# A hybrid attention block on one core: the MLP's two-operand work moves to VectorE, squares to ScalarE, and what is spilled to DRAM is laid out anew

## The chip, the cores and the metric

The kernel runs on one core of one Trainium2 chip. The metric is the device time of one execution in microseconds (us), lower is better. Five engines matter: TensorE (PE in the profile, its weight loads PEld), VectorE (DVE), ScalarE (ACT), GpSimd (POOL) and SyncE (SP), which issues nearly all DMA transfers. Each works through its own queue in order and waits on semaphores for the others.

## What is computed

A sequence of 1024 rows of width 1024 goes through one layer in float32: a mixer (sparse attention heads and gated DeltaNet heads), and then an MLP with a norm on either side. The change lies in the MLP and in the turning of its input:

```python
D_MODEL = 1024; SEQ = 1024; D_FF = 4 * D_MODEL
def rms_norm(x, g):
    y = x * lax.rsqrt(jnp.mean(x * x, axis=-1, keepdims=True) + EPS)
    return y * g
...
    x = x + rms_norm(mix, post_norm_mix[l])
    h = rms_norm(x, pre_norm_mlp[l])
    y = jnp.square(jax.nn.relu(h @ w_mlp_in[l])) @ w_mlp_out[l]
    x = x + rms_norm(y, post_norm_mlp[l])
```

## The kernel before

Products are made of split numbers: a float32 operand becomes a high part (a cast to a shorter type, by ScalarE) and a low part (what the cast left, a subtraction by VectorE or GpSimd, `parts`, L1414 to L1421), and one product is three matmuls, high by high, high by low, low by high (`mm3`, L192 to L201).

**The input turned.** `turn_h2` (L1365) takes each block of 128 rows of x after the mixer, multiplies it by its row's factor (L1375), turns it with eight transposes into two PSUM banks, and writes high and low parts of h, the norm's weight being applied per partition in the same step (L1386, L1387). h lies transposed in `h2H` and `h2L`. It is one of several generators that a small planner (`Flow`) interleaves with the end of the mixer; the blocks come from the last to the first. The order on each engine's queue is then set by a scheduler that simulates the program, and not by the order of the text alone.

**Four plain blocks.** 4 of the 32 blocks of 128 hidden columns are done plainly (`plain`, L1472): 24 matmuls for each half of the rows, a squared Relu (`squared`, L1465), a write to DRAM.

**28 blocks in 14 pairs.** The others go through a scheme of seven products of blocks in place of eight. It needs sums and differences of the four quarters of h: `turns_of_h` (L1487) adds high and low parts of h back together in spare tiles, forms three combinations (b11, b22, b21) with their high and low parts in `TH` and `TL`, and a fourth that replaces a half of h. The first loop (L1559) takes the pairs in turn. For each, `left_parts` (L1522) forms the four sums of weight quarters and the parts of seven left sides, at most three or four combinations ahead; then, in the order 1, 5, 6, 2, 7, 3, 4, come 12 matmuls a combination, and the results are added up, squared and combined. Seven blocks of 256 KB a pair are written to `hid_d` (`spill`).

The second loop (L1686) multiplies these by w_mlp_out. It takes the pairs in chunks of 2, 3, 3, 3 and 3, and for each chunk the combinations 1, 2, 5, 3, 6, 7, 4: a step. `both_parts` (L1635) reads the hidden blocks into spare tiles, forms the differences of weight quarters, and makes the parts of both sides, in rings of 12 buffers (`hq` for the hidden side, `hl` for the weights). A step of a triple is 36 matmuls, four row blocks t by three pairs, and after each row block `gather` (L1676) adds a PSUM bank to an accumulator. Raw weights of a chunk (1 MB a pair) are loaded at the chunk's start. Most of the memory of the second loop is that of h and its sums, so `room` (L1617) opens it when the first loop is through.

At the end the accumulator u is added to three others (L1714), the four plain blocks are multiplied (L1735), and `finish` norms each row block and adds x.

## Time and profile before

| | |
|---|---|
| median of 3 runs | 1456.03 us (1451.3 to 1461.72) |
| the profiled execution | 1456.56 us, its span 1454.9 us |
| instructions | 20267 |
| TensorE busy | 1310.5 us, 6643 matmuls |
| VectorE busy | 1102.6 us |
| ScalarE busy | 684.0 us |
| GpSimd busy | 754.3 us |
| mean granted clock of TensorE | 0.945 of full |
| DMA | 180.29 MB, mean 124 GB/s |

The span runs from the first to the last instruction of one execution; places in it are given in us from its start. Busy shares are means over the whole span. The MLP's products run from about 763 us (beside the end of the mixer) to 1437 us. A stretch is judged by how many matmuls it issues, since a matmul's busy time overlaps with the next one's.

### The profile page before, as it was taken

The numbers are of one execution on the slowest core, as the hardware profiler recorded it, in microseconds if no ns is written. First come the engines' busy times: TensorE is split into PE (matmuls) and PEld (weight loads), VectorE is DVE, ScalarE is ACT, GpSimd is POOL, SyncE is SP. The second block draws the span as 40 slices with busy tenths as digits, with TensorE's granted clock in tenths as the row PEclk, the third lists the DMA queues.
The fourth block names the chain that finished last, engine by engine and source line by source line (L and its number), as shares of the span: only waits on it lengthen the run. The fifth ranks groups of instructions, "written<-read, shape, count | busy, mean of one in ns | idle before, by whom it ended". The sixth has DMA issues, their size and how long they took to land. (4 is left out here: it accounts for less than half of the span.)

```text
span 1454.9 us, 20267 instructions
## 1 busy us (share of the span) xinstructions
PE 1310.5 (90%) x6643; PEld 1120.7 (77%) x6643; DVE 1102.6 (76%) x2350; ACT 684.0 (47%) x1475; POOL 754.3 (52%) x625
## 2 busy tenths in 40 slices
PE   7898997988876999999989599999994999999995
PEld 5687885877765999878877488888883888887874
DVE  5524759998997898997786957777776877767946
ACT  5433336777632677776464333333331443434422
POOL 3163320222233434348011846777663999899973
PEclk8999998999985999999999799999997999999998
DMA  6222112555163332334435124444447645543015
GB/s 186 69 70 80 44 30 58 172 150 127 44 165 103 102 92 72 113 109 153 148 130 174 46 96 156 159 152 156 152 155 278 236 125 172 181 129 110 30 55 177
DMA packets 159939, 180.29 MB, mean 124 GB/s; under 512 B 26129, under 2 KB 113370, under 8 KB 159706
## 3 DMA queue, kind: packets, MB, share of 16 engines
q1 hardware_dynamic: 159834, 179.00, 39.2%
q8 instruction: 52, 0.85, 0.3%
q14 instruction: 53, 0.43, 0.1%
HBM read 120.76 MB, written 59.78 MB: 124 GB/s over the span
## 5 line engine op out<-in xcount | busy, mean ns | idle before, releaser
L199 PE MATMUL two<-hTH,wh 128*128 128x512 f32 (+1 forms) x416 | 165.9, 401 | 26.0 <-ACT tmp L424 16.0
L200 PE MATMUL two<-hTL,wh 128*128 128x512 f32 (+1 forms) x416 | 166.1, 399 | 0.0
L201 PE MATMUL two<-hTH,wl 128*128 128x512 f32 (+1 forms) x416 | 164.8, 397 | 0.0
L1420 POOL TENSOR_TENSOR hq<-tmp,hq 128x512 fp32r<-128x512 f32 x96 | 143.9, 1513 | 9.8 <-ACT hq L1419 8.4
L1420 POOL TENSOR_TENSOR hl<-raw,hl 128x512 fp32r<-128x512 f32 x67 | 100.7, 1513 | 51.9 <-ACT hl L1419 51.9
L1419 ACT CAST hq<-tmp 128x512 fp32r<-128x512 f32 x96 | 59.1, 617 | 128.3 <-POOL hq L1420 67.0
L269 POOL TENSOR_SCALAR wh<-stg 128x1024 fp32r<-128x1024 f32 x19 | 19.9, 1046 | 191.1 <-PE two L200 191.1
L199 PEld LDWEIGHTS two<-hTH,wh 128*128 128x128 f32 (+1 forms) x416 | 81.8, 197 | 43.6 <-issue 22.7
L521 ACT ACTIVATE jk<-score,cand 128x1024 bf16<-128x1024 f32 (+2 forms) x96 | 92.5, 966 | 45.1 <-DVE cand L532 31.4
L1419 ACT CAST hl<-tmp 128x512 fp32r<-128x512 f32 x58 | 35.6, 618 | 160.7 <-DVE tmp L1535 60.9
L201 PEld LDWEIGHTS two<-hTH,wl 128*128 128x128 f32 (+1 forms) x416 | 81.6, 196 | 12.7 <-issue 0.9
L200 PEld LDWEIGHTS two<-hTL,wh 128*128 128x128 f32 (+1 forms) x416 | 81.8, 197 | 12.0 <-issue 0.7
L270 POOL TENSOR_TENSOR wl<-stg,wh 128x1024 fp32r<-128x1024 f32 (+1 forms) x26 | 60.8, 2340 | 54.1 <-ACT wh L267 52.6
L1134 POOL TENSOR_TENSOR mt<-tz,maskb 128x256 f32<-128x256 f32 x56 | 38.4, 691 | 60.4 <-DVE mx L1150 39.6
L1158 ACT ACTIVATE big<-big,nm 128x256 f32<-128x256 f32 (+6 forms) x64 | 50.6, 791 | 12.5 <-DVE nm L1157 12.5
L199 PE MATMUL acc<-h2H,hl 128*128 128x512 f32 x120 | 47.5, 400 | 9.1 <-DVE tmp L1469 9.1
L1419 ACT CAST hl<-raw 128x512 fp32r<-128x512 f32 x88 | 52.8, 615 | 5.4 <-PE acc L200 4.9
L1184 DVE TENSOR_TENSOR part<-tr,part 128x512 fp32r<-128x512 f32 x80 | 50.2, 630 | 4.9 <-ACT part L1183 4.6
L1183 ACT CAST part<-tr 128x512 fp32r<-128x512 f32 x80 | 43.2, 542 | 20.6 <-PE tr L1181 17.1
L200 PE MATMUL acc<-h2L,hl 128*128 128x512 f32 x120 | 47.7, 398 | 4.5 <-DVE h2L L1387 4.5
L1206 PE MATMUL acc<-part,VS 128*128 128x256 f32 x288 | 49.4, 295 | 1.3 <-DVE part L1184 1.2
L587 DVE SCALAR_TENSOR_TENSOR tmp<-two,svT,tmp 128x1023 f32<-128x1023 f32 (+2 forms) x36 | 45.5, 1276 | 4.0 <-ACT tmp L585 3.0
(516 smaller groups left out, 4385.7 us busy)
## 6 DMA issues: line engine op xcount, KB each, us to landing
hid_d<-tmp SPq DMA_DIRECT2D x98, 256.0 KB, 2.0
tmp<-hid_d SPq DMA_DIRECT2D x98, 256.0 KB, 2.7
raw<-in_w_mlp_in_dram SPq DMA_DIRECT2D x14, 1024.0 KB, 8.2
raw<-in_w_mlp_out_dram SPq DMA_DIRECT2D x14, 1024.0 KB, 5.1
stg<-in_w_in_dram SPq DMA_DIRECT2D x25, 512.0 KB, 4.1
x<-in_x_dram SPq DMA_DIRECT2D x8, 512.0 KB, 5.5
la_d<-la SPq DMA_DIRECT2D x8, 512.0 KB, 3.7
q<-qa_d SPq DMA_DIRECT2D x64, 64.0 KB, 2.4
```

The source lines that it names most:

```text
L199: PE.matmul(o, lh, rh, start=start, stop=False, skip_group_check=more)
L200: PE.matmul(o, lh, rl, start=False, stop=False, skip_group_check=more)
L201: PE.matmul(o, ll, rh, start=False, stop=stop, skip_group_check=more)
L270: G.tensor_sub(wl[:, :, :n], f[:, :, :n], wh[:, :, :n].bitcast(F32))
L521: S.activation(junk[:, :n], s_of(b), AF.Sign, bias=cand[:, 3 + i:4 + i].bitcast(F32), scale=-1.0, accum_out=cnt[:, 3 + i:4 + i])
L587: V.scalar_tensor_tensor(acc[:, 3 - j:T], both[:, 0:T - 3 + j], w[j], acc[:, 3 - j:T], op0=OP.mult, op1=OP.add)
L1158: S.activation(pr[:, :n], pr[:, :n], AF.Exp, bias=nm, accum_out=den[:, hh:hh + 1])
L1183: S.copy(pt[:, 0:2 * nj, 0, :], v4(ps)[:, 0:2 * nj])
L1184: V.tensor_sub(pt[:, 0:2 * nj, 1, :], v4(ps)[:, 0:2 * nj], pt[:, 0:2 * nj, 0, :].bitcast(F32))
L1206: PE.matmul(po[:, hh * 256:hh * 256 + 256], VS[:, j + a, 2 * p + hh, :], pt[:, 2 * a + hh].rearrange("p a t -> p (a t)"), start=j + a + hh ...
L1419: S.copy(h_, src)
L1420: eng.tensor_sub(l_, src, h_.bitcast(F32))
```

## The change

Names of the parts, in the order of the text:

- `turn_h2`: the norm's weight is applied to rows, ahead of the transposes, in one operation with two tensor inputs on VectorE (a tile `gain` holds the weights in every partition). Parts are then taken from four transposed blocks at once. A plain copy of them, `hf`, is made by ScalarE and written to DRAM, in four tiles (two halves of the columns by two halves of the rows).
- `turns_of_h` reads these blocks from DRAM in place of adding high and low parts; its low parts go to VectorE.
- `squared` and the other squares: Relu and then Square on ScalarE.
- Every `parts`, addition and subtraction of the two loops and of the closing rows that was on GpSimd goes to VectorE, with the first three plain weight loads and `finish` left as they were.
- `hid_d`: one DRAM tile for each pair and combination; combinations 1, 2 and 4 are split before they are written, high and low part, and read straight into the ring `hq` (`hl` for the very first).
- Raw weights of the next chunk are loaded at combinations 3 and 6 of the current one, and the third after it.
- The additions of u come within the last chunk, after combinations 6, 7 and 4, row block by row block.

```diff
@@ -1372,20 +1372,19 @@
             yield flow.now + 3.0
-        V.tensor_scalar(xr, xr, r2[:, tb:tb + 1], None, op0=OP.mult)
-        yield dve(flow.now, 1.1)
+        V.scalar_tensor_tensor(xr, xr, r2[:, tb:tb + 1], h2["gain"], op0=OP.mult, op1=OP.mult)
+        yield dve(flow.now, 1.3)
...
             yield from bank("tr")
...
-            for k in range(4):
-                kk = kh * 4 + k
-                ts_ = slice(tb * P, (tb + 1) * P)
-                gn = svT[:, 57 + kk:58 + kk]
-                S.activation(h2["H"][:, kk, ts_], ps[:, k * P:(k + 1) * P], AF.Identity, scale=gn)
-                V.scalar_tensor_tensor(h2["L"][:, kk, ts_], ps[:, k * P:(k + 1) * P], gn,
-                                       h2["H"][:, kk, ts_].bitcast(F32), op0=OP.mult, op1=OP.subtract)
+            kk, ts_ = slice(4 * kh, 4 * kh + 4), slice(tb * P, (tb + 1) * P)
+            S.copy(h2["H"][:, kk, ts_], v4(ps))
+            V.tensor_sub(h2["L"][:, kk, ts_], v4(ps), h2["H"][:, kk, ts_].bitcast(F32))
+            hf = pl.t(h2["hf"], H4, F32, "hf", bufs=2)
+            S.copy(hf, v4(ps))
+            SY.dma_start(h2["d"][kh][tb // 4][:, :, tb % 4 * P:tb % 4 * P + P], hf)
...
             yield 0.0
@@ -1406,6 +1405,10 @@
+h2["hf"], hf_close = pl.open("hf")
+h2["gain"] = pl.t(h2["hf"], [P, D], F32, "gmlp")
+SY.dma_start(h2["gain"], bcast(pre_norm_mlp, P))
+h2["d"] = [[pl.t(dram, [P, 4, 512], F32, f"h2_d{i}{j}") for j in range(2)] for i in range(2)]
@@ -1420,13 +1423,13 @@
-def load_plain(f, stage, **kw):
+def load_plain(f, stage, eng, **kw):
...
-    mlp[f] = [parts(raw[:, 4 * k:4 * k + 4, :], G) for k in range(2)]
+    mlp[f] = [parts(raw[:, 4 * k:4 * k + 4, :], eng) for k in range(2)]
...
-    load_plain(f, pool["wk"], bufs=2)
+    load_plain(f, pool["wk"], G, bufs=2)
@@ -1434,6 +1437,7 @@
+hf_close()
@@ -1448,8 +1452,9 @@
-hid_d = pl.t(dram, [NP2, 7, P, 512], F32, "hid_d")
-plain_d = pl.t(dram, [NS, P, T], F32, "plain_d")
+hid_d = {(i, j): pl.t(dram, [P, 512], F32, f"hid{i}_{j}") for i in range(NP2) for j in range(3, 7)}
+hid_d.update({(i, j): pl.t(dram, [P, 2, 512], F32, f"hid{i}_{j}") for i in range(NP2) for j in range(3)})
+plain_d = [pl.t(dram, [P, T], F32, f"plain{f}") for f in range(NS)]
...
 def tmp(dtype=F32):
@@ -1466,12 +1471,12 @@
-    V.scalar_tensor_tensor(r, ps, 0.0, r, op0=OP.max, op1=OP.mult)
+    S.activation(r, r, AF.Square)
...
 def plain(f, th):
...
-        load_plain(f, stg)
+        load_plain(f, stg, V)
@@ -1479,25 +1484,24 @@
-    SY.dma_start(plain_d[f, :, sl], r)
+    SY.dma_start(plain_d[f][:, sl], r)
...
 def turns_of_h(k):
...
-    f = {}
-    for i, (kk, sl) in enumerate(((k, LO), (k, HI), (k + 4, LO), (k + 4, HI))):
-        f[i] = tmp()
-        (G if i % 2 else V).tensor_tensor(f[i], hTH[:, kk, sl].bitcast(F32), hTL[:, kk, sl].bitcast(F32), OP.add)
-    b11, b12, b21, b22 = f[0], f[1], f[2], f[3]
+    f = [tmp() for _ in range(4)]
+    for i in range(4):
+        SY.dma_start(f[i], h2["d"][i // 2][i % 2][:, k])
+    b11, b12, b21, b22 = f
...
-        G.tensor_sub(TL[:, j, k], t, TH[:, j, k].bitcast(F32))
+        V.tensor_sub(TL[:, j, k], t, TH[:, j, k].bitcast(F32))
@@ -1527,20 +1531,20 @@
     def t3d():
...
-    yield 1, parts(a11, G)
+    yield 1, parts(a11, V)
...
-    G.tensor_add(s1, a21, a22)
-    yield 5, parts(s1, G)
+    V.tensor_add(s1, a21, a22)
+    yield 5, parts(s1, V)
...
     yield 6, parts(s2, V)
-    yield 2, parts(a12, G)
+    yield 2, parts(a12, V)
...
-    G.tensor_sub(s3, a11, a21)
+    V.tensor_sub(s3, a11, a21)
     yield 7, parts(s3, V)
...
     yield 3, parts(s2, V)
-    yield 4, parts(a22, G)
+    yield 4, parts(a22, V)
@@ -1551,7 +1555,15 @@
 def spill(i, j, t):
-    SY.dma_start(hid_d[i, j], t)
+    if j > 2:
+        SY.dma_start(hid_d[i, j], t)
+        return
+    hi = tmp(F32R)
+    S.copy(hi, t)
+    V.tensor_sub(t.bitcast(F32R), t, hi.bitcast(F32))
+    SY.dma_start(hid_d[i, j][:, 0], hi.bitcast(F32))
+    SY.dma_start(hid_d[i, j][:, 1], t)
@@ -1575,43 +1587,44 @@
     elif j == 2:
-        r11 = t_["r11"] = squared(ps)
-        spill(i, 0, r11)
+        t_["r11"] = squared(ps)
     elif j == 7:
...
-        G.tensor_mul(r22, r22, r22)
+        S.activation(r22, r22, AF.Square)
...
-        spill(i, 3, r22)
     elif j == 3:
...
-        V.tensor_mul(r12, r12, r12)
+        S.activation(r12, r12, AF.Square)
...
-        G.tensor_add(s1, r12, t_["r22"])
+        V.tensor_add(s1, r12, t_["r22"])
...
+        spill(i, 2, t_["r22"])
...
-        G.tensor_sub(r12, t_["r11"], r12)
+        V.tensor_sub(r12, t_["r11"], r12)
...
+        spill(i, 0, t_["r11"])
...
     elif j == 4:
...
-        V.scalar_tensor_tensor(r21, r21, 0.0, r21, op0=OP.max, op1=OP.mult)
-        spill(i, 1, r21)
+        S.activation(r21, r21, AF.Relu)
+        S.activation(r21, r21, AF.Square)
...
-        spill(i, 2, s4)
+        spill(i, 3, s4)
+        spill(i, 1, r21)
...
-WHICH = {1: 0, 2: 1, 3: 2, 4: 3, 5: 4, 6: 5, 7: 6}
+WHICH = {1: 0, 2: 1, 4: 2, 3: 3, 5: 4, 6: 5, 7: 6}
...
 def room():
@@ -1636,8 +1649,15 @@
     for i in chunks[c]:
-        f = tmp()
-        SY.dma_start(f, hid_d[i, WHICH[j]])
+        own = (hlp, "hl") if c == 0 and j == 1 else (rooms["hq"], "hq")
+        if WHICH[j] < 3:
+            h = tuple(pl.t(own[0], [P, 512], F32R, own[1]) for _ in range(2))
+            for a in range(2):
+                SY.dma_start(h[a].bitcast(F32), hid_d[i, WHICH[j]][:, a])
+        else:
+            f = tmp()
+            SY.dma_start(f, hid_d[i, WHICH[j]])
+            h = parts(f, V, *own)
...
         if j == 5:
@@ -1651,23 +1671,26 @@
         elif j == 7:
...
-            G.tensor_sub(t, b22, b12)
+            V.tensor_sub(t, b22, b12)
...
-        h = parts(f, G, *((hlp, "hl") if c == 0 and j == 1 else (rooms["hq"], "hq")))
-        w = parts(t, V if i % 2 else G)
-        res.append((h, w))
+        res.append((h, parts(t, V)))
...
 def sides():
...
+    for i in chunks[0]:
+        raws[i] = raw_out(i, rawp)
...
-        for i in ch:
-            raws[i] = raw_out(i, rooms["raw"] if c else rawp)
         for j in ORDER:
+            if j in (3, 6) and c + 1 < len(chunks):
+                i = chunks[c + 1][(3, 6).index(j)]
+                raws[i] = raw_out(i, rooms["raw"])
...
             yield c, j, both_parts(c, j, raws, ts)
+        if c + 1 < len(chunks):
+            raws[chunks[c + 1][2]] = raw_out(chunks[c + 1][2], rooms["raw"])
@@ -1697,8 +1720,11 @@
-        for name in {1: ("u",), 2: ("11",), 5: ("22",), 3: ("12",), 6: ("u",), 7: ("22",), 4: ("21",)}[j]:
-            gather(name, t, ps)
+        name = {1: "u", 2: "11", 5: "22", 3: "12", 6: "u", 7: "22", 4: "21"}[j]
+        gather(name, t, ps)
+        if c + 1 == len(chunks) and j in (6, 7, 4):
+            a = acc["12" if j == 6 else name][:, t]
+            V.tensor_add(a, a, acc["u"][:, t])
@@ -1707,15 +1733,10 @@
-    G.tensor_sub(hq[:, 1], r, hq[:, 0].bitcast(F32))
+    V.tensor_sub(hq[:, 1], r, hq[:, 0].bitcast(F32))
...
-    rows.append((hq, [parts(raw[:, sl], G, *((hlp, "hl") if f < 2 else (rooms["hq"], "hq"))) for sl in (LO, HI)]))
-for name in ("12", "22", "21"):
-    for t in range(4):
-        a = acc[name][:, t]
-        (V if name == "12" else G).tensor_add(a, a, acc["u"][:, t])
+    rows.append((hq, [parts(raw[:, sl], V, *((hlp, "hl") if f < 2 else (rooms["hq"], "hq"))) for sl in (LO, HI)]))
 def finish(tb, yt):
```

## Rows read from the trace of the kernel before

**Rows 1.** The page of the profile: busy time, share of the span and instructions of the engines, and the granted clock of TensorE in 40 equal slices of the span, in tenths of full speed.

```profile
PE 1310.5 (90%) x6643; PEld 1120.7 (77%) x6643; DVE 1102.6 (76%) x2350; ACT 684.0 (47%) x1475; POOL 754.3 (52%) x625
...
PEclk8999998999985999999999799999997999999998
```

**Rows 2.** A table by stretch of the MLP: the stretch and its length, busy time and number of instructions of PE, PEld, DVE, ACT and POOL, the granted clock, the DMA engines' busy share, GB/s.

```profile
801.00:849.20 48.20, 32.34 (x128) 26.21 (x129) 40.11 (x40) 16.49 (x30) 35.45 (x23) 0.82 0.15 49
849.20:1107.70 258.50, 255.04 (x1165) 218.59 (x1163) 189.95 (x206) 86.60 (x152) 172.89 (x122) 1.00 0.44 153
1107.70:1140.00 32.30, 11.79 (x39) 8.99 (x39) 16.27 (x17) 8.81 (x16) 19.44 (x14) 0.68 0.99 374
1140.00:1315.00 175.00, 175.00 (x813) 153.24 (x812) 137.98 (x157) 73.50 (x135) 163.82 (x112) 1.00 0.49 153
1315.00:1341.00 26.00, 23.73 (x104) 18.96 (x103) 18.42 (x21) 9.25 (x18) 26.00 (x19) 1.00 0.37 109
...
1375.00:1403.50 28.50, 25.18 (x106) 20.54 (x105) 12.34 (x15) 5.63 (x10) 28.04 (x21) 0.94 0.11 38
1403.50:1437.30 33.80, 33.74 (x157) 29.20 (x155) 25.30 (x59) 10.23 (x32) 16.82 (x14) 1.00 0.41 139
1437.30:1454.90 17.60, 0.00 (x0) 0.00 (x0) 9.17 (x22) 2.58 (x8) 3.87 (x3) 0.59 0.44 153
```

**Rows 3.** TensorE in order of time ahead of the first loop: start, duration, line, operation and tiles, and in brackets the idle time before it and what ended it. Only the last four transposes, the rows with long idle times and the first product on a block sum are shown.

```profile
798.86 0.60 PE L1381 MATMUL tr<-ident,stg 128*128 128x128 f32 x4
...
809.44 0.79 PE L200 MATMUL acc<-h2L,hl 128*128 128x512 f32 x1 [4.06 <-DVE h2L L1387]
...
822.11 0.80 PE L199 MATMUL ch<-h2H,hl 128*128 128x512 f32 x1 [4.81 <-ACT hl L1419]
...
829.90 0.79 PE L199 MATMUL acc<-h2H,hl 128*128 128x512 f32 x1 [6.57 <-DVE tmp L1469]
...
849.22 0.38 PE L199 MATMUL sc<-TH,hl 128*128 128x512 f32 x1
```

**Rows 4.** VectorE and GpSimd in order of time in the same stretch, the columns as above.

```profile
818.62 1.72 POOL L1420 TENSOR_TENSOR hl<-stg,hl 128x512 fp32r<-128x512 f32 x1
819.13 1.75 DVE L1496 TENSOR_TENSOR tmp<-tmp,tmp 128x512 f32<-128x512 f32 x1
820.30 5.05 POOL L1500 TENSOR_TENSOR TL<-tmp,TH 128x512 fp32r<-128x512 f32 x3
820.81 1.75 DVE L1492 TENSOR_TENSOR tmp<-h2H,h2L 128x512 f32<-128x512 f32 x1
```

**Rows 5.** Groups of instructions of one line and shape: count, busy us and mean ns of one, and the idle time before them with what ended it. All but the last are of the first loop, the last is of the second.

```profile
L1592 DVE TENSOR_TENSOR tmp<-tmp 128x512 f32<-128x512 f32 x13 | 9.0, 692 | 9.0 <-ACT tmp L1591 9.0
...
L1594 POOL TENSOR_TENSOR tmp<-tmp,tmp 128x512 f32<-128x512 f32 x13 | 16.6, 1273 | 15.4 <-DVE tmp L1592 12.8 <-issue 2.5
...
L1535 DVE TENSOR_TENSOR tmp<-tmp,raw 128x512 f32<-128x512 f32 x13 | 23.0, 1766 | 0.0
...
L1598 POOL TENSOR_TENSOR tmp<-tmp,tmp 128x512 f32<-128x512 f32 x13 | 23.2, 1781 | 1.0
...
L1583 ACT ACTIVATE tmp<-tmp 128x512 f32<-128x512 f32 x14 | 8.8, 625 | 4.1 <-DVE tmp L1582 4.1
...
L1681 DVE TENSOR_TENSOR acc<-acc,acc 128x512 f32<-128x512 f32 x22 | 14.8, 682 | 10.6 <-PE acc L201 10.6
```

**Rows 6.** VectorE in order of time, late in the second loop.

```profile
1352.24 0.68 DVE L1420 TENSOR_TENSOR hl<-raw,hl 128x512 fp32r<-128x512 f32 x1
1352.84 0.67 DVE L1681 TENSOR_TENSOR acc<-acc,tr 128x512 f32<-128x512 f32 x1
```

**Rows 7.** SyncE between the two loops, in order of time (a row with a count stands for that many issues from its start on), and the first product of the second loop.

```profile
1107.86 0.90 SPq L1632 DMA_DIRECT2D raw<-in_w_mlp_out_dram  x2
...
1109.32 1.69 SPq L1632 DMA_DIRECT2D raw<-in_w_mlp_out_dram  x3
...
1118.79 16.15 SPq L1640 DMA_DIRECT2D tmp<-hid_d  x19
...
1127.12 1.22 PE L199 MATMUL ch<-hl,hl 128*128 128x512 f32 x2 [19.28 <-ACT hl L1419]
```

**Rows 8.** DMA traffic of 1110 to 1130 us (the first three rows) and of 1150 to 1200 us (the last): what moved, and by kind of transfer the number, size and median us from issue to landing.

```profile
DMA packets 2936, 8.03 MB, mean 401 GB/s; under 512 B 255, under 2 KB 255, under 8 KB 2936
...
tmp<-hid_d SPq DMA_DIRECT2D x13, 256.0 KB, 5.3
...
hid_d<-tmp SPq DMA_DIRECT2D x4, 256.0 KB, 10.9
...
tmp<-hid_d SPq DMA_DIRECT2D x20, 256.0 KB, 2.7
```

**Rows 9.** TensorE late in the second loop and at its end, rows with an idle time.

```profile
1325.53 0.45 PE L199 MATMUL sc<-hl,hq 128*128 128x512 f32 x1 [0.86 <-ACT hl L1419]
...
1337.68 0.48 PE L200 MATMUL ch<-hl,hq 128*128 128x512 f32 x1 [0.95 <-POOL hl L1420]
...
1399.45 0.67 PE L200 MATMUL ch<-hl,raw 128*128 128x512 f32 x1 [1.89 <-POOL hl L1420]
```

**Rows 10.** Groups of instructions: the third matmul of combination 6 in the first loop, and VectorE's part of the turning of h between 700 and 860 us.

```profile
L201 PE MATMUL tr<-TH,hl 128*128 128x512 f32 x52 | 21.1, 405 | 1.9 <-DVE hl L1420 1.9
...
L1387 DVE SCALAR_TENSOR_TENSOR h2L<-tr,svT,h2H 128x128 fp32r<-128x128 f32 x64 | 20.7, 344 | 8.1 <-ACT h2H L1386 8.1
```

## The prediction

> **What bounds the kernel now.** I read the busy shares and the granted clock over the span first. TensorE is the busiest engine (1310.5 us of 1454.9) and its clock falls from full to half only in a few slices [rows 1]. So the second view is a table by stretch of the MLP, the only part that the change touches apart from the turning of its input. The reader is to see there how many products a stretch issues. In the undisturbed part of the second loop 813 products take 175.0 us, 0.2155 us each, and TensorE does not rest [rows 2]. That is the floor of a product here, and every other stretch is measured against it:
> - 801 to 849.2 us: 128 products take 48.2 us where 27.6 would do. 20.6 us lost.
> - 849.2 to 1107.7 us, the first loop: 84 products for each of 14 pairs less 12 before the window make 1164, 250.8 us at the floor, in 258.5. 7.7 us lost.
> - 1107.7 to 1140: 39 products, 8.4 us, in 32.3. 23.9 us lost.
> - 1315 to 1341: 104 products, 22.4 us, in 26.0. 3.6 us lost.
> - 1375 to 1403.5: 106 products, 22.8 us, in 28.5. 5.7 us lost.
> After 1437.3 no product is left; 17.6 us of tail [rows 2].
>
> So the loops are at TensorE's bound, and what the MLP can give is 61.5 us in five places. Who ends each wait is read from the rows of TensorE that carry an idle time. Ahead of the first loop VectorE ends two of three waits (4.06 and 6.57 us), ScalarE behind it the third (4.81), and the first product that needs a block sum starts at 849.22 [rows 3]. In that stretch VectorE and GpSimd run side by side and one 128x512 operation takes 1.72 to 1.75 us on either [rows 4]. The same operation takes 0.692 us on VectorE where GpSimd rests (squaring r12 in place), 1.273 us on GpSimd where VectorE rests, and 1.766 and 1.781 us where they meet; one input in PSUM leaves it at 0.682 [rows 5]. Alone, VectorE starts one every 0.60 us [rows 6].
>
> **Fewer hands, shorter queue.** The change gives VectorE GpSimd's share. First loop, one pair: VectorE has 15 operations now, 23 after (11 for the weights, 12 for the results, three of them the new low parts). 23 x 0.60 = 13.8 us, beside 84 x 0.2155 = 18.1 us of TensorE. ScalarE gets 19 operations of about 0.62 [rows 5], 11.8 us. Second loop, a triple: 28 gathers, 12 low parts of hidden blocks (21 less 9 that come split), 21 of weights, 12 differences, 73 x 0.60 = 43.8 us against 252 x 0.2155 = 54.3. Even at the full 0.69 each (50.4) VectorE stays under TensorE. So the loops keep TensorE's pace: no gain there but for the stalls, no loss.
>
> The trace speaks against sharing work between the two. The Trainium skill ("Perfetto Trace Analysis", Optimizing Scalar/DVE Operations) advises to hand work to ScalarE or even GpSimd where VectorE is saturated, though it adds that those two share a read port; by its first half alone the move is a mistake and all terms below would be nought or worse. The page "SBUF — State Buffer" (Who interferes with whom) says that a VectorE instruction with two SBUF inputs and a GpSimd one that reads SBUF hold each other up for the whole instruction, which the 1.75 us rows bear out.
>
> **Term A, ahead of the first loop.** Removed: 16 additions that rebuild h from its parts, half of them on GpSimd, and 12 low parts on GpSimd; the square in `squared` goes to ScalarE, so a PSUM bank is free after one Relu and no longer waits behind VectorE's queue, which is what the 6.57 us were. Added: 16 copies on ScalarE, 16 writes and 16 reads of 256 KB. When does the last block sum come? The last transposes end at 799.5 [rows 3]; two copies of 0.6, a write of about 2.5 (no row has this form; the nearest is 2.7 for a read of the same size [rows 8], and 512-byte pieces may cost more), a first pair of reads of 2.7: 806. From there 28 operations on VectorE plus seven for weights, 35 x 0.60 = 21.0: 827. TensorE has 128 products to issue from 801, until 828.6, and now nothing of theirs waits for VectorE. The reads of the half that was turned first can go before. So the first product on a block sum starts at about 830 for 849.2: **-19 us**. Bounds: -23, if the wait and slow clock before 801 go as well; -11, if the reads land late, as the 5.3 us in the crowded stretch [rows 8], and a few microseconds of waiting drop the clock again.
> Turning itself: eight operations of 0.344 us on VectorE per half block [rows 10] become two of 0.69 and half a wide one of two inputs (about 1.3, estimated as twice 0.69): little less per block. **-1**, bounds -3 to +1.
>
> **Term B, within the first loop.** The third product of combination 6 waits for a low part on VectorE, 1.9 us in all, and the clock-independent hitches beside it make the rest of the 7.7 us [rows 10]. VectorE's 1.77 us operations ahead of it in the queue shrink to 0.69. **-5**, bounds -7.7 and 0 (the order of VectorE's queue can leave a wait).
>
> **Term C, between the loops.** SyncE issues five loads of w_mlp_out of 1 MB at 1107.9 to 1111, ahead of the reads of hidden blocks, most of which follow from 1118.8; the first product of the second loop starts at 1127.12 after 19.28 us without work [rows 7]. In 1110 to 1130 the queue moves 8.03 MB at 401 GB/s, a read lands after 5.3 us, a spill after 10.9 [rows 8]. After: a hidden block is a tile of its own, so a read waits only for its own writes and can go before the last spills; the blocks of combination 1 come split, so two steps on ScalarE and GpSimd are gone; the loads for the next triple are written behind the reads of combinations 5 and 3. What is late next: the weights of the second raw tile (1 MB, some 5 us after the last pair's parts) and VectorE, which at the seam has 11 operations of the last pair left, then 10 gathers and parts a step: 25 x 0.60 = 15 us until combination 5 starts, for about 13 of TensorE. I take 2 to 3 us of each, 5 in all, for 23.9 lost now: **-19**. Bounds: -23; -10, if the five loads are pulled ahead of the reads again, since that order is not the program's own.
>
> **Term D, late.** The waits at 1325.53 and 1337.68 end with ScalarE and GpSimd [rows 9]; GpSimd's queue is gone: **-4** (bounds -4 and 0). At the end VectorE takes over 8 of 12 additions of u (all 12 now fall within the last triple) and 12 low parts for the plain rows: 12 x 0.60 + 8 x 0.60 + 4 x 1.2 = 16.8 us more, in a triple with 54.3 - 43.8 = 10.5 us to spare. About 6 us late, for the 5.7 lost today, where the last wait ends with GpSimd [rows 9]: **-1**, bounds -5 and +5. The tail keeps its form: 0.
>
> **Term E, direct reads.** The split blocks land in the ring of 12 that TensorE reads, which comes free only when a combination two steps back is done. Before, they landed in spare tiles far ahead. Six reads have the 7.8 us of one step (36 x 0.2155): five issues at 0.45 us (two took 0.90 [rows 7]) and a landing of 2.7 [rows 8] make 5.0. Hidden, with 2.8 us of slack. At 14 such steps I allow **+2**, bounds 0 and +8. Spilling 10 blocks for 7 a pair adds traffic only: 3.7 MB in 18.1 us, 204 GB/s, half of what the queue moved at its fullest.
>
> **Sum.** -19 - 1 - 5 - 19 - 4 - 1 + 2 = -47 from the profiled execution, 1456.56 us (span 1454.9 and 1.7 around it; the median of three is 1456.03): about 1410, given as 1411. With every term at its good end -66, at its bad end -9; the good ends do not all come at once, since a wait removed in one queue shows another.
>
> **Rivals.**
> - *The seams only shrink.* Reads that wait for writes replace the additions ahead of the loop and the five loads still jam the seam: A -11, C -10, B 0, late +2, E +2: about 1439. For it: both seams hang on an order that SyncE's queue gets and the program does not state. Against it: the first reads need no other wait.
> - *The direct reads come late.* With landings of 10.9 us, as the spills had in the jam [rows 8], and an issue every 0.85 us (19 in 16.15 [rows 7]), a step would be 10.9 + 4.3 - 7.8 = 7.4 us late, 14 times 104 us, in place of the 2 above: near 1512. From 3.4 us late per step (48 over 14) the kernel is slower than before. Against it: outside the jam a read takes 2.7 us [rows 8], and the mean load stays near 200 GB/s.
> - *It does not do what it says.* TensorE's waits may hang on the queue order, not on VectorE's time; then the seams stay and only small terms come: about 1450.
>
> **How the numbers follow.** One per cent is 14.6 us, about what a measurement of this kernel can tell. Forecast 0.70 (1396 to 1432), shrunk seams 0.14, no effect 0.10, late reads 0.06. A range of 1396 to 1446 holds the first case and most of the second. Faster by over 1% (below 1441.5) takes the forecast and most of the shrunk seams, 0.82; within 1% 0.10; slower 0.08, the late reads and a tail of the third.
>
> **What would show it.** Right: the first product on a block sum some 19 us earlier; VectorE's two-input operations at 0.69 us throughout and GpSimd nearly idle in the MLP; under 8 us between the loops; no clock loss at either seam; products in the second loop still 0.2155 us apart. Wrong: TensorE waiting for a DMA into the ring at combinations 4, 1 or 2; VectorE busy without a pause in the last triple and TensorE waiting for it; a first read between the loops that follows 1 MB loads again.

## The result, and the profile after

The changed kernel takes 1416.62 us (median of four, 1410.68 to 1417.32) against 1455.01 before: a ratio of 0.972, 95% interval 0.968 to 0.977. The forecast was 1411 us, with a range of 1396 to 1446. The profiled execution took 1417.32 us, with a span of 1415.6; 39.3 us of span are gone, where the sum said 47.

The page of the changed kernel, the lines that answer to [rows 1]:

```profile
PE 1299.8 (92%) x6643; PEld 1120.9 (79%) x6643; DVE 1104.6 (78%) x2551; ACT 730.1 (52%) x1521; POOL 272.0 (19%) x296
...
PEclk8899998999995899999999899999999899999998
```

TensorE issues the same 6643 matmuls. VectorE runs 201 instructions more in 2.0 us more of busy time (1102.6 before): what it took over from GpSimd costs it almost no busy time, because its own operations got shorter. The table by stretch, columns as in [rows 2]:

```profile
785.00:832.80 47.80, 39.56 (x170) 32.67 (x168) 26.73 (x46) 21.99 (x43) 0.00 (x0) 0.89 0.70 232
832.80:1086.90 254.10, 254.06 (x1175) 221.97 (x1176) 193.47 (x312) 149.37 (x260) 0.00 (x0) 1.00 0.58 201
1086.90:1120.00 33.10, 19.84 (x72) 16.09 (x71) 27.98 (x46) 13.88 (x25) 0.00 (x0) 0.74 0.96 360
1120.00:1285.00 165.00, 165.00 (x766) 144.50 (x765) 139.85 (x227) 56.81 (x100) 0.00 (x0) 1.00 0.62 207
...
1300.16:1354.55 54.39, 54.39 (x253) 47.63 (x252) 48.66 (x78) 20.88 (x36) 0.00 (x0) 1.00 0.27 88
...
1366.00:1398.00 32.00, 32.00 (x149) 27.78 (x147) 22.85 (x59) 9.58 (x32) 16.38 (x13) 1.00 0.44 148
```

Both loops now run at TensorE's pace to the end (766 in 165.0 us, 0.2154 each; 149 in 32.0). The row from 1300.16 on is the last triple of the second loop, of 252 matmuls. In the first loop VectorE does 312 operations in 193.5 us, where 206 took 190.0 [rows 2]. Two groups of it, to be read beside [rows 5]:

```profile
L1423 DVE TENSOR_TENSOR hl<-tmp,hl 128x512 fp32r<-128x512 f32 x51 | 34.8, 683 | 0.9
...
L1564 DVE TENSOR_TENSOR tmp<-tmp,tmp 128x512 fp32r<-128x512 f32 x39 | 26.7, 685 | 1.4
```

What is left are five waits, three ahead of the first loop and two between the loops. TensorE in order of time, rows with an idle time:

```profile
805.41 0.79 PE L199 MATMUL ch<-h2H,hl 128*128 128x512 f32 x1 [2.21 <-ACT hl L1422]
810.57 0.79 PE L201 MATMUL ch<-h2H,hl 128*128 128x512 f32 x1 [3.94 <-DVE hl L1423]
832.81 0.48 PE L199 MATMUL sc<-TH,hl 128*128 128x512 f32 x1 [1.85 <-ACT hl L1422]
...
1095.83 0.77 PE L199 MATMUL ch<-hl,hq 128*128 128x512 f32 x1 [5.89 <-ACT hl L1422]
1110.09 0.80 PE L199 MATMUL sc<-hl,hq 128*128 128x512 f32 x1 [7.37 <-ACT hq L1422]
```

The first product on a block sum starts at 832.81 (849.22 before [rows 3]). Between the loops two stalls of 5.89 and 7.37 us stand in place of one of 19.28 [rows 7]. SyncE there still issues the five 1 MB loads ahead of the unsplit hidden blocks:

```profile
1075.22 2.81 SPq L1656 DMA_DIRECT2D hl<-hid  x3
...
1091.62 0.60 SPq L1645 DMA_DIRECT2D raw<-in_w_mlp_out_dram  x1
...
1093.00 2.50 SPq L1645 DMA_DIRECT2D raw<-in_w_mlp_out_dram  x4
1095.55 1.33 SPq L1659 DMA_DIRECT2D tmp<-hid  x2
```

### The profile page after: what moved, and what is told of

The parts are those of the page before. It is cut to its first block, busy times and chain, and to the rows that moved or that the text cites. A ratio compares the mean times of both kernels' runs of the same rounds, so it can differ in the third digit from the quotient of the medians.

```text
span 1415.6 us, 20269 instructions
## 1 busy us (share of the span) xinstructions
PE 1299.8 (92%) x6643; PEld 1120.9 (79%) x6643; DVE 1104.6 (78%) x2551; ACT 730.1 (52%) x1521; POOL 272.0 (19%) x296
## 5 line engine op out<-in xcount | busy, mean ns | idle before, releaser
L1750 POOL TENSOR_TENSOR tmp<-acc,c_row 128x512 f32<-128x512 f32 x16 | 20.7, 1302 | 644.3 <-DVE acc L1763 635.3
L1422 ACT CAST hq<-tmp 128x512 fp32r<-128x512 f32 x56 | 34.4, 616 | 79.5 <-PE tr L200 39.0
L1423 DVE TENSOR_TENSOR hl<-raw,hl 128x512 fp32r<-128x512 f32 x88 | 59.6, 685 | 7.3 <-ACT hl L1422 7.1
L1422 ACT CAST hl<-tt 128x512 fp32r<-128x512 f32 x56 | 34.5, 615 | 31.1 <-PE tr L200 16.5
L199 PE MATMUL sc<-hl,hq 128*128 128x512 f32 x112 | 42.7, 390 | 7.4 <-ACT hq L1422 7.4
```

Source lines behind the costliest of these rows:

```text
L199: PE.matmul(o, lh, rh, start=start, stop=False, skip_group_check=more)
L1422: S.copy(h_, src)
L1423: eng.tensor_sub(l_, src, h_.bitcast(F32))
```

## The experiments

Every run has its own loss by stage, which says more than its time. TensorE's matmuls are counted from the program's start; from the start of one numbered matmul to that of another, less 0.2157 us for each (their spacing where nothing waits), is the time lost. The 3800th to the 4150th is the stretch ahead of the first loop and its first products, to the 5000th the first loop, to the 5600th the seam between the loops, from there to the last the second loop. The stretch ahead of these, 3000th to 3800th, took 137 to 145 us from profile to profile, between kernels that are alike there too (138.3 in the changed kernel, 142.3 with the loads held back; the granted clock of 660 to 700 us was 1.00 in the one and 0.96 in the other). So a difference of 4 us between two times can be nothing, and the stages decide. They come from one profile a kernel and scatter too: ahead of the first loop five kernels that are alike there (changed, e1, e2, e7, e11) lose 6.0 to 9.8 us, at the seam three (changed, e3, e4) 16.1 to 18.2. The ratio is to the kernel before on the same chip.

| kernel | ahead | first loop | seam | second loop | time, us | ratio, 95% interval |
|---|---|---|---|---|---|---|
| before | 24.2 | 4.1 | 25.7 | 10.0 | 1455 to 1460 | 1 |
| changed | 9.3 | 0.3 | 18.2 | 0.1 | 1416.62 | 0.972 (0.968 to 0.977) |
| e6 engines alone | 5.0 | 0.1 | 22.0 | 0.1 | 1420.99 | 0.974 (0.972 to 0.977) |
| e5 GpSimd in the loops | 7.1 | 8.9 | 23.1 | 0.1 | 1426.73 | 0.978 (0.975 to 0.981) |
| e10 GpSimd outside them | 11.8 | 0.1 | 16.8 | 2.0 | 1418.13 | 0.972 (0.970 to 0.975) |
| e13 GpSimd everywhere | 15.6 | 8.9 | 21.8 | 7.0 | 1445.05 | 0.992 (0.989 to 0.995) |
| e4 sums added | 2.8 | 0.3 | 16.1 | 0.1 | 1412.02 | 0.968 (0.965 to 0.971) |
| e3 plain block on GpSimd | 6.6 | 0.4 | 17.9 | 0.1 | 1416.07 | 0.972 (0.969 to 0.974) |
| e7 no split | 6.0 | 0.1 | 22.4 | 0.1 | 1422.47 | 0.976 (0.972 to 0.980) |
| e11 one tile | 7.9 | 0.3 | 15.4 | 0.1 | 1414.59 | 0.970 (0.966 to 0.974) |
| e1 loads held | 9.8 | 0.3 | 11.8 | 0.1 | 1413.07 | 0.969 (0.966 to 0.972) |
| e2 copies on ScalarE | 6.8 | 0.3 | 15.4 | 0.1 | 1410.96 | 0.970 (0.967 to 0.973) |
| e9 e1, e2 and e3 | 6.3 | 0.4 | 18.5 | 0.1 | 1413.22 | 0.972 (0.968 to 0.975) |
| e12 reads in order | 2.8 | 0.3 | 3.9 | 2.0 | 1399.79 | 0.960 (0.956 to 0.964) |

**Which part made the gain: the engines.** The kernel before with the engines changed alone (every `G.` of the two loops and the closing rows to `V.`, the squares to `S.activation`; the first three plain weight loads and `finish` as they were):

> The kernel before with only the engines changed: every two-operand operation of the last stage on VectorE, every square on ScalarE, the last plain block's parts on VectorE. One DRAM tile for the hidden combinations, no splits, block sums added from the parts, the turned norm weights and the order of the loads stay as before. My theory: losses inside the first loop and late in the second go (7.7 and 9.3 us), part of the loss ahead of the first loop too, the seam keeps its 24 us or more: about 1432. Rival, that the gain hangs on the DRAM tiles and splits: within 5 us of the kernel before, about 1452.

1420.99 us: nearly the whole gain, and 11 us more of it than expected. The loss ahead of the first loop fell further than with the full change (5.0 against 9.3; in it are two waits of 1.96 and 3.17 us for the old turning's low part, L1387), the seam less (22.0 against 18.2). The first product on a block sum comes no earlier (833.77 us, 832.81 in the changed kernel), because TensorE gets there later: the 3500th to the 3800th matmul, beside the turning, take 62.7 us in this run, 64.3 in the kernel before, and 59.4 to 60.9 in all twelve kernels with the new turning. The other way round, GpSimd's share given back to the changed kernel, in the loops first:

```
-        yield 1, parts(a11, V)
+        yield 1, parts(a11, G)
...
-            V.tensor_sub(r12, t_["r11"], r12)
+            G.tensor_sub(r12, t_["r11"], r12)
...
-                h = parts(f, V, *own)
+                h = parts(f, G, *own)
```

> The changed kernel with GpSimd's old share given back in both loops: the low parts of four of the first loop's seven combinations, two of its sums, one sum and one difference of each hidden pair, the low parts of hidden blocks, half of those of the second matrix. The tiles in DRAM, the splits, the direct block sums and the squares on ScalarE stay as changed. My theory, that the engines sharing work made the losses inside the first loop (7.7 us), and late in the second (9.3 us): they come back, and the time rises by 12 to 17 us, to about 1430. Rival, that the tiles of their own in DRAM and the splits did it: the time stays within 3 us of the changed kernel.

The first loop's loss came back, at 8.9 us more than twice the 4.1 of the kernel before; the late one did not (0.1): half of the theory held. The seam lost 23.1, some 5 more than the changed kernel, which the theory did not have. Groups of that run in the first loop, columns as in [rows 5]:

```profile
L1609 POOL TENSOR_TENSOR tmp<-tmp,tmp 128x512 f32<-128x512 f32 x12 | 21.4, 1783 | 0.9
...
L1607 DVE TENSOR_TENSOR tmp<-tmp,tmp 128x512 f32<-128x512 f32 x12 | 21.2, 1767 | 0.0
...
L1586 DVE TENSOR_TENSOR tmp<-tr,tmp 128x512 f32<-128x512 f32 x12 | 8.1, 677 | 0.0
```

Where the two meet, VectorE's operation with two inputs in SBUF takes 1.77 us again, GpSimd's beside it 1.78; one with an input in PSUM stays at 0.68. Then GpSimd's share outside the loops, on the kernel with added sums (e4 below):

```
-            V.tensor_sub(TL[:, j, k], t, TH[:, j, k].bitcast(F32))
+            G.tensor_sub(TL[:, j, k], t, TH[:, j, k].bitcast(F32))
...
-        V.tensor_sub(hq[:, 1], r, hq[:, 0].bitcast(F32))
+        G.tensor_sub(hq[:, 1], r, hq[:, 0].bitcast(F32))
```

> The changed kernel with its block sums added from the parts (as in the run where they were added on VectorE), and GpSimd's old share given back only outside the two loops: half of those additions, the low parts of the turned sums and of the last plain block ahead of the first loop; in the closing rows the low parts and all but one group of the last additions. With GpSimd back inside both loops the losses ahead of the first loop and late in the second had stayed away. My theory now, that these two losses belong to exactly these operations: TensorE loses 15 us or more again ahead of the first product on a block sum (2.9 us from its 3800th to its 4150th matmul with the sums on VectorE, 24.3 in the kernel before), and some 10 us late in the second loop (0.1 against 10.0), the first loop and the seam staying as they are: about 1434. Rival, that the late loss came from the seam or the reads of the old layout, and that VectorE's share alone matters ahead: under 5 us in all, about 1415.

9.0 us came back ahead of the first loop, where 15 or more were expected, and 1.9 late where 10 were: neither theory. The table by stretch gave the next one; here it is for the last 113 us of TensorE's work, in the kernel before:

```profile
1285.00:1398.00 113.00, 108.87 (x494) 92.16 (x492) 85.27 (x91) 44.64 (x80) 109.56 (x72) 1.00 0.25 77
```

and in the run with GpSimd in the loops (e5), the run with GpSimd outside them (e10), and the one with both (e13), one after the other:

```profile
1285.00:1398.00 113.00, 113.00 (x526) 98.94 (x525) 95.75 (x136) 39.18 (x76) 61.98 (x41) 1.00 0.36 119
```

```profile
1285.00:1398.00 113.00, 111.08 (x512) 96.05 (x510) 82.70 (x144) 35.35 (x75) 47.91 (x35) 1.00 0.34 112
```

```profile
1285.00:1398.00 113.00, 108.92 (x493) 93.78 (x493) 77.02 (x95) 38.59 (x72) 93.60 (x63) 0.98 0.30 101
```

The fifth pair of figures is GpSimd. It was busy for 109.56 of 113 us before, for 61.98 and 47.91 with a part of its share (16.80 in the changed kernel, where the norms of `finish` are left to it).

> GpSimd's whole old share given back at once: inside both loops and outside them, with the block sums added from the parts. DRAM tiles, splits and the squares on ScalarE stay as changed. With its share in the loops alone the second loop lost 0.1 us late, with its share outside them alone 2.0; the kernel before lost 10.0. My theory, from GpSimd's busy time in the last 113 us of the second loop (109.6 us in the kernel before, 62.0 and 47.9 us in the two runs with a part of its share): the late loss is a GpSimd that is full, so the two shares together bring back 7 to 11 us there where neither did alone; the first loop loses some 9 us, the stretch ahead of it 12 to 24, and the time is about 1440. Rival, that the late loss hung on the old reads or on the squares on VectorE: the second loop loses under 3 us, time about 1428.

With both shares the second loop lost 7.0 us, neither alone more than 2.0, and the time rose to 1445.05. TensorE's longest wait there ends with GpSimd, which had worked without a pause since 1340.87 us:

```profile
1381.82 0.48 PE L200 MATMUL ch<-hl,raw 128*128 128x512 f32 x1 [1.95 <-POOL hl L1420]
```

So the late loss takes both shares at once, and a full GpSimd explains it; the other long wait (1.31 us at 1376.15) stands behind a load of w_mlp_out, and why that load was late was not followed. Against the same kernel without GpSimd (e4, 1412.02) its share costs 33 us.

**Ahead of the first loop: the direct sums cost time.** The copies, writes and reads of h are replaced by additions (the copy `hf` and its write in `turn_h2` go too):

```
...
-        for i in range(4):
-            SY.dma_start(f[i], h2["d"][i // 2][i % 2][:, k])
+        for i, (kk, sl) in enumerate(((k, LO), (k, HI), (k + 4, LO), (k + 4, HI))):
+            V.tensor_tensor(f[i], hTH[:, kk, sl].bitcast(F32), hTL[:, kk, sl].bitcast(F32), OP.add)
```

> The changed kernel with the sixteen block-sum operands rebuilt by adding high and low parts on VectorE, as before, in place of the copies, the writes to DRAM and the sixteen reads. My theory, that the reads at the end of the turning (issued from 799.47 on, over 11.5 us) hold VectorE's and ScalarE's queues as long as sixteen more additions of some 0.6 us would: the first product on a block sum moves by less than 3 us from 832.8, and the time by less than 3 us. Rival, that the direct reads carry the gain ahead of the first loop (16.4 us): the time rises by 8 us or more.

Neither: it got no slower, and the first product on a block sum starts earlier:

```profile
825.23 0.48 PE L199 MATMUL sc<-TH,hl 128*128 128x512 f32 x1 [2.14 <-ACT hl L1419]
```

7.6 us earlier than with the reads, and the loss ahead is 2.8 for 9.3 (2.8 in e12 too, which has the same additions). The 4.6 us between the two times are not clear of the noise by themselves. VectorE in the changed kernel shows why, in order of time:

```profile
802.93 0.69 DVE L1498 TENSOR_TENSOR tmp<-tmp,tmp 128x512 f32<-128x512 f32 x1 [6.29 <-DMA tmp<-h_d]
...
808.01 0.69 DVE L1499 TENSOR_TENSOR tmp<-tmp,tmp 128x512 f32<-128x512 f32 x1 [2.97 <-DMA tmp<-h_d]
808.62 0.69 DVE L1423 TENSOR_TENSOR hl<-stg,hl 128x512 fp32r<-128x512 f32 x1
809.23 0.68 DVE L1500 TENSOR_TENSOR tmp<-tmp,tmp 128x512 f32<-128x512 f32 x1
809.83 0.68 DVE L1423 TENSOR_TENSOR hl<-raw,hl 128x512 fp32r<-128x512 f32 x1
```

It stands still for 6.29 and 2.97 us on reads, and the low part that TensorE waits for until 810.57 (that of the first pair's combination 1, `hl<-raw`, from 809.83 to 810.51) is queued behind them. Sixteen additions of 0.69 us fill that time. A part of the gain can be TensorE's order, which changed with it: combination 1 comes at 805.41 in the changed kernel, ahead of 72 matmuls of the plain blocks, and at 820.34, behind them, in this run. The low part at 808.62, that of the plain block (`hl<-stg`), on GpSimd instead (`load_plain(f, stg, G)`):

> The changed kernel with the low parts of the last plain block of the first pair made on GpSimd again, in place of VectorE. My theory, that ahead of the first loop they stand on VectorE behind operations that wait for the block sums' reads from DRAM (PE idle 3.94 us at 810.57, released by VectorE): that stall goes and the time falls by 2 to 5 us, to about 1413. Rival, that the queues of ScalarE and the reads set the first product on a block sum at 832.8 whatever comes before it, so that the stall comes back behind: same time within 1.5 us, the gap moving to the wait ahead of 832.8.

The rival held: the time is the same, and the first product on a block sum starts at 832.79. The edit moved another low part than the one that TensorE waits for, which still stands on VectorE behind the reads:

```profile
810.01 0.68 DVE L1423 TENSOR_TENSOR hl<-raw,hl 128x512 fp32r<-128x512 f32 x1
```

```profile
810.75 0.79 PE L201 MATMUL ch<-h2H,hl 128*128 128x512 f32 x1 [2.84 <-DVE hl L1423]
```

The 2.7 us less that the table gives to the stage are only TensorE's later arrival there: the last transposes start at 794.3 us in this profile, at 791.6 in the changed kernel's.

**The seam: tiles, splits, loads, copies.** All combinations in one DRAM tile again, split ones still split:

```
-    hid_d = {(i, j): pl.t(dram, [P, 512], F32, f"hid{i}_{j}") for i in range(NP2) for j in range(3, 7)}
-    hid_d.update({(i, j): pl.t(dram, [P, 2, 512], F32, f"hid{i}_{j}") for i in range(NP2) for j in range(3)})
+    hid_d = pl.t(dram, [NP2, 10, P, 512], F32, "hid_d")
```

> The changed kernel with all hidden combinations in one DRAM tile again, the split ones still written and read as two parts; everything else as changed. My theory, that a read waits only for the write of its own region and that the tiles of their own do nothing by themselves: the first product of the second loop still starts ahead of the first loop's end, time within 2 us of the changed kernel. Rival, that with one tile the reads wait for the latest write of any combination: the overlap at the seam is gone (a gap of some 20 us as without the splits) and the time rises by 4 us or more.

No loss; the first split reads leave about as early (1076.41 us, 1075.22 in the changed kernel). The tiles of the hidden blocks do nothing by themselves. No combination split (`spill` writes each block once, `both_parts` makes its two parts after the read):

> The changed kernel with every hidden combination written once as a 256 KB block and made into its two parts after it is read, none split ahead; the tiles in DRAM stay one each. My theory: the splits move three VectorE and three ScalarE operations per pair from the second loop to the first, where neither engine is full, and the queue at the seam is the same or shorter without them: within 3 us of the changed kernel, rather faster. Rival, that the direct reads keep the second loop fed: the late losses (9.3 us) come back at least in part, and the time rises by 4 us or more.

My theory fell: the seam loses 22.4 for 18.2, and the time is 5.9 us longer (the intervals of the two ratios overlap). The rival had the size, but not the place: the second loop loses 0.1. TensorE and SyncE of that run:

```profile
1104.56 1.22 PE L199 MATMUL ch<-hl,hl 128*128 128x512 f32 x2 [19.47 <-ACT hl L1422]
```

```profile
1090.62 0.50 SPq L1646 DMA_DIRECT2D tmp<-hid  x1
...
1096.39 3.50 SPq L1646 DMA_DIRECT2D tmp<-hid  x3
```

The old stall of 19.5 us is back, because the first hidden blocks are read at 1090.62 and 1096.39, behind the 1 MB loads, where the split ones leave at 1075.22. Next, the five loads behind the latest unsplit read:

```
-        SY.dma_start(raw, w_mlp_out[r0:r0 + 256, :].rearrange("(a p) d -> p a d", p=P))
+        with (tc.issue_after(behind) if behind is not None else ExitStack()):
+            SY.dma_start(raw, w_mlp_out[r0:r0 + 256, :].rearrange("(a p) d -> p a d", p=P))
```

> The changed kernel with one thing different: on SyncE's queue the next chunks' 1 MB loads of the out matrix stand behind the latest read of an unsplit hidden block, so that they no longer all go out ahead of the first reads of the second loop. My theory, that the second stall of the seam (PE idle 7.37 us at 1110.09, ScalarE there waiting 4.57 us for a hidden block) is made by those five loads: that stall goes to under 2 us, the reads there land in some 3 us in place of 5.3, and the time falls by 5 to 9 us, to about 1409. Rival, that VectorE's full queue at the seam holds the parts back and the loads only look guilty: the stall moves by a few us and the time stays within 2 us of the changed kernel, about 1416.

The stall of 7.37 us went and the seam lost 6.4 us less, as expected, but not because the unsplit reads landed sooner: they took 7.2 us where some 3 were expected, and left earlier, between the loads. Another stall came, for a read of a split block:

```profile
1130.18 0.45 PE L199 MATMUL sc<-hl,hq 128*128 128x512 f32 x1 [3.08 <-DMA hq<-hid]
```

The time, 1413.07, can't be told from 1416.62 by itself. Then the gather's first copies on ScalarE (`S.copy(a, ps)` for `V.tensor_copy(a, ps)`):

> The changed kernel with the sixteen first-time copies of the gather (from a product's bank into the sums) on ScalarE in place of VectorE. My theory, that the first stall of the seam (PE idle 5.89 us at 1095.83) is VectorE's backlog, its copies of the gather queued behind the last combinations of the first loop: the stall shrinks to 0 to 3 us and the time falls by 2 to 5 us, to about 1413. Rival, that the stall waits for the parts of the raw rows (loaded only at 1086) or for a hidden block, whoever copies: unchanged stall and a time within 1.5 us of the changed kernel.

```profile
1088.03 0.48 PE L199 MATMUL ch<-hl,hq 128*128 128x512 f32 x1 [1.96 <-ACT acc_u L1707]
...
1104.89 0.80 PE L199 MATMUL sc<-hl,hq 128*128 128x512 f32 x1 [11.41 <-ACT hq L1422]
```

The first stall shrank from 5.89 to 1.96 us, but the second grew from 7.37 to 11.41: what was won was given back at once. The 2.8 us that the stage lost less, about what the seam scatters, lie in the clock after the stalls, which was granted at 0.88, 0.61 and 1.00 in the three stretches of 10 us from 1090 on, where the changed kernel had 0.66, 0.78 and 0.71. And all three:

> The changed kernel with the three edits together: the out matrix's loads behind the reads, the gather's first copies on ScalarE, the last plain block's low parts on GpSimd. My theory, that the three stalls are separate: the sum of the three single gains, 9 to 17 us, a time of about 1403, below both kernels. Rival, that all of them are faces of one full VectorE or of one late transfer: the three together give no more than the best of them alone.

Not the sum of the gains (1413.22 us, where 1403 were expected): the seam lost 18.5 us, as in the changed kernel. TensorE in that run:

```profile
1126.57 0.76 PE L199 MATMUL sc<-hl,hq 128*128 128x512 f32 x1 [10.34 <-DMA hq<-hid]
```

One transfer ends this wait, a split block's. DMA traffic of the changed kernel from 1085 to 1140 us, columns as in [rows 8]:

```profile
DMA packets 9236, 20.13 MB, mean 366 GB/s; under 512 B 955, under 2 KB 955, under 8 KB 9235
...
tmp<-hid SPq DMA_DIRECT2D x25, 256.0 KB, 5.4
raw<-in_w_mlp_out_dram SPq DMA_DIRECT2D x5, 1024.0 KB, 12.0
hq<-hid SPq DMA_DIRECT2D x16, 256.0 KB, 5.3
```

Unsplit reads need only one of 17 spare tiles and run up to 25 ahead; split ones need a place in the ring that TensorE reads and are issued when it comes free, behind all that. In both runs with the loads held back this was the next stall. So the last kernel has the sums added, the copies on ScalarE, and each of the second stage's loads behind the one before it in the order of use:

```
+    def read(dst, src):
+        with (tc.issue_after(last[0]) if last else ExitStack()):
+            last[0] = SY.dma_start(dst, src).ins
```

> The changed kernel with three edits: the block sums added on VectorE, the gather's first copies on ScalarE, and every load of the second loop and of the closing rows (1 MB loads, split and unsplit hidden blocks) on SyncE's queue in the order in which the products want them. The runs with the 1 MB loads held back still stopped 3.5 and 10.7 us for a split block, whose read stood behind up to 25 unsplit ones while 16 DMA engines moved some 400 GB/s. My theory, that the seam's last stall is the order of the transfers and not their sum: the seam loses under 9 us (18.2 in the changed kernel) and the time is about 1402, below every kernel so far. Rival, that in order a read that waits for a free buffer holds up the first loop's writes or the 1 MB loads behind it, or that the bytes are simply too many: the seam loses 15 us or more, 1410 or above.

1399.79 us, a ratio of 0.960, the lowest of all. Stretches of it, and SyncE:

```profile
1090.00:1100.00 10.00, 7.73 (x35) 6.00 (x34) 8.49 (x14) 6.10 (x13) 0.00 (x0) 1.00 1.00 358
1100.00:1120.00 20.00, 20.00 (x94) 17.51 (x93) 14.96 (x24) 10.24 (x19) 0.00 (x0) 1.00 0.79 277
```

```profile
1088.68 0.41 SPq L1643 DMA_DIRECT2D raw<-in_w_mlp_out_dram  x1
...
1101.64 3.18 SPq L1643 DMA_DIRECT2D hq<-hid  x4
1104.88 0.42 SPq L1643 DMA_DIRECT2D raw<-in_w_mlp_out_dram  x1
1106.17 16.21 SPq L1643 DMA_DIRECT2D hq<-hid  x12
```

The split reads (hq) leave from 1101.64 on, between single 1 MB loads; with the three edits before they left at 1119.86. The queue moves 277 GB/s in 1100 to 1120 and TensorE does not rest; the seam loses 3.9 us. Neither of the other two edits alone takes it below 15.4 (e2; 16.1 in e4), but the two together without the order were not run. The second loop loses 2.0 us, most of it where TensorE's matmul of a closing row starts at 1346.83, after a wait of 1.17 us for this cast, and the cast for a load that SyncE issued at 1342.61:

```profile
1346.16 1.14 ACT L1419 CAST hq<-raw 128x512 fp32r<-128x512 f32 x2 [4.31 <-DMA raw<-in_w_mlp_out_dram]
```

So the order costs something there: the closing rows' loads were held back too.

## Why the prediction was right, and where it was off

Of its signs, VectorE's 0.69 us, GpSimd at rest and the spacing of the products in the second loop came as written, and the first product on a block sum nearly so. Two did not: the seam lost 18.2 us and not under 8, and the clock fell at both seams (0.89 granted over 785 to 832.8, 0.74 over 1086.9 to 1120). That the time still lay 6 us from the forecast is in part luck: most of what the seam fell short by was made up late in the second loop and in the turning, whose gains were put too small.

- **VectorE alone is as fast as the two together.** Right: 0.68 to 0.69 us throughout, GpSimd at 0.00 in the first loop and in the second to the end of its last triple. The rate of one operation each 0.60 us was read where GpSimd was in fact at work [rows 6]; the changed kernel shows it where GpSimd rests (809.23 to 809.83 above), and the 13.8 us of VectorE forecast for a pair are what it took (193.47 over 14). The Trainium skill ("Perfetto Trace Analysis", Optimizing Scalar/DVE Operations) says that handing work of a saturated VectorE to GpSimd may make sense, and that between these two it might not help, as they share a read port. Here the second holds: in this kernel sharing costs 33 us (e13 against e4).
- **A, forecast -19, was -16.4** by the first product on a block sum (832.81; some 830 were forecast), -14.9 by the stage's loss. The size held, its working only in part. Engines alone lose 5.0 us there, the full change 9.3, and with additions in place of the reads 2.8, so the direct reads were no gain: reads that land late were the bound of this term (-11), and the step "now nothing of theirs waits for VectorE" failed, since VectorE's own queue waited for the reads and TensorE 3.94 us for VectorE. GpSimd everywhere brings the stage from 2.8 (e4) back to 15.6 (e13), of 24.2 before. Of the other 8.6, 4.06 were the wait for the old turning's low part [rows 3], which no kernel with the new turning has; the rest, the squares among it, was not tried.
- **Turning, forecast -1, was -3.9** by the 300 matmuls beside it (64.3 to 60.4 us, 3500th to 3800th). The kernels with the new turning lie within 1.5 us of one another there (59.4 to 60.9), and the engines alone, with the old one, at 62.7, so some 2 us at the least are the turning's own.
- **B, forecast -5, was -3.8** by the matmuls (4.1 to 0.3), -6.8 by the windows that the prediction used (7.7 to 0.9, which is 254.1 less 1175 x 0.2155). Right, and e5 shows the cause.
- **C, forecast -19, was -7.5** (25.7 to 18.2): the mis-sized term. Two waits make 13.3 of the 18.2 us, most of the rest is the clock. The prediction named the condition of its own bound, -10 if the five loads are pulled ahead of the reads again; they were (1091.62 to 1095.5, the first unsplit read at 1095.55), as its last paragraph said would show it wrong. What it lacked is the rest: VectorE's backlog was more than the 2 to 3 us allowed, as the gather's first copy comes at 1095.05; and reads of two kinds in one queue with different numbers of free buffers overtake each other. The tile for each block, which it counted on, does nothing (e11); the splits do 4.2 us (e7), by leaving early.
- **D, forecast -4 and -1, was -9.9.** The end was mis-sized: VectorE was to be some 6 us late in the last triple, and TensorE did not wait once. The triple's 252 matmuls took 54.4 us, and VectorE was busy for 48.66 of them with 78 operations, where the prediction put 60.6 us of work: a part of it ran outside the triple, 3 of the 12 additions of u and 2 of the 4 wide low parts of the plain rows among it. Both shares of GpSimd together bring 7.0 us of the late loss back (e13).
- **E, forecast +2, was 0** in the second loop. The reads into the ring land after 5.3 us in the crowded stretch and hold up only the seam.

The sum of the forecast, -47, and the -39.3 measured differ by 7.7: C gave 11.5 less, A 4.1 less, B 1.2 less, D 4.9 more, E 2 more, the turning 2.9 more, and 0.7 less is left, within the scatter of the stretches ahead. The bad ends of the prediction's terms add up to -7, not to the -9 that it gives; its range does not hang on that.

## What to carry to other kernels

Before work is shared between VectorE and GpSimd, compare one operation's time on each alone with its time where they meet. Where both rise as here (0.69 to 1.77 us on VectorE, 1.27 to 1.78 on GpSimd), the two do two operations in the 1.8 us in which VectorE alone does nearly three (one each 0.60 us), and its queue is no shorter for the sharing. Where loads of several kinds share one queue, put them in the order of use: a kind with many free buffers otherwise runs ahead and delays the one that the products want next. After a stall is removed, name the next one and its transfer before counting the gain.

## What the runs showed of the hardware

VectorE, with GpSimd at rest, did 312 operations in 193.5 us beside TensorE, where it needed 190.0 for 206 with GpSimd at work, as was forecast. That an operation with one input in PSUM is untouched by a busy GpSimd, as the prediction read from [rows 5], held with GpSimd's share given back (e5: 0.677 us beside 1.767 for one with two in SBUF). This agrees with the Trainium skill ("SBUF — State Buffer", Who interferes with whom), which says that an instruction of VectorE with two SBUF inputs contends with GpSimd's reads, and that one with at most one, outside the 2-port modes, does not. And the DMA engines kept a mean of 391 GB/s from 1100 to 1140 us at the seam, while a 256 KB read took 5.3 to 5.4 us to land, where it took 2.7 outside the crowd [rows 8].
